# One 512-column product per weight for both parts of x in the input projections, the halves summed on evacuation, and some of VectorE's steps on ScalarE

## The chip, the cores and the metric

The kernel runs on one core of a Trainium2 chip. A core has TensorE for matrix products (into PSUM, 8 banks of 512 fp32 columns), VectorE, ScalarE and GpSimd for the rest, and DMA queues, of which SyncE drives the one that loads weights. The metric is the device time of one execution in microseconds, smaller being better; given is the median of the runs.

## The reference

Two layers over 256 rows of 1024 columns. Each layer projects the rows once, runs three mixers on slices of that projection, projects their joined outputs back, adds and normalises, and then runs a mixture of 32 experts:

```python
def hybrid_mixer(x, w_in, ...):
    p = x @ w_in
    s_z, s_xbc, s_dt, rw, gq, gk, gv, gg, ga = _split(p, IN_SPLITS)
    y_ssd = ssd_mixer(s_z, s_xbc, s_dt, ...)
    y_rwkv = rwkv7_mixer(rw, ...)
    y_gla = gla_mixer(gq, gk, gv, gg, ga, ...)
    y = jnp.concatenate([y_ssd, y_rwkv, y_gla], axis=-1).astype(x.dtype)
    return y @ w_out
...
    for i in range(DEPTH):
        mix = hybrid_mixer(h, w_in[i], ...)
        h = layer_norm(DEEPNORM_ALPHA * h + mix, ln1_g[i], ln1_b[i])
        ffn = hierarchical_moe(h, ...)
        h = layer_norm(DEEPNORM_ALPHA * h + ffn, ln2_g[i], ln2_b[i])
```

The ssd mixer runs a short convolution over its slice (`xbc`) and then a chunked scan with decays exp(min(a_i − a_j, 0)); the rwkv mixer a delta rule, whose chunks are solved with a Neumann series of 32x32 blocks; the gla mixer linear attention with decays from a log sigmoid divided by 16.

## The kernel before

All is fp32, and the products of the mixer keep nearly fp32's accuracy with fp32r operands: each operand is split in a high and a low part (`hi`, a copy on ScalarE rounded to fp32r, and `lo`, the difference, on VectorE), and three products, hi·hi, hi·lo and lo·hi, add up in one PSUM tile (`mm3`, lines 437 to 439). For the rows x, transposed, this is done once a layer (`transposed`, tiles `xh` and `xl`). For a weight it is done in pieces of 128x1024, the tiles `wparts`: the cast on ScalarE (line 143, where every ScalarE operation is recorded) and the difference on VectorE (L411). Three pieces are prepared ahead (`NA`), and there are five buffers (`hring`).

The mixer of a layer is written as three streams of work. Stream r is the rwkv mixer, which starts with the projections lrq and k. Stream s, called attend, holds the gates and decays of the other two (`prep`), the ssd scan (`ssd`, `ssd_out`) and the linear attention (`linear`). Stream d holds the other projections in the order r, v, bc, x0, x1, gk, gv, gg, z0, z1 (`dense`), and then the four output projections (`out_proj`), each of which works in 512 columns. A hand-written clock takes turns between the streams, by the cost that each `yield` states; on the order so written a scheduler lays its own. The result is one fixed order for each engine, with the streams' steps mixed; each engine works through its own order and waits at an instruction until its operands are there.

A projection (`proj`, L542) computes 256 output channels as two halves m of 128, each with 8 steps of 128 inputs; weight pieces are stationary and x moves, 256 columns at a time. Both halves go to one PSUM bank. Halves are read from there by `shift` (L565, the token shift), by `conv` (one ScalarE step and three VectorE steps, L888, for each half), by the gates, or by a copy. For gv the roles are turned: x is stationary and the weights move. The first half of lrq is done apart, in 24 products in another order (L551); it is not touched. The PSUM banks are dealt by stream: three for r, three for d, two for s.

The names that come up later: L659 and L661 form the matrix of the Neumann series; L662 to L665 mask and transpose it into `TM` and `TA`; L765 and L770 are the products of the series, 64 blocks of 32x32 each, with `XY` (L766) and `TM` (L771, L772) evacuated between them on VectorE. L967 and L968 are the cumulative sums of ssd's decays, from `adt`; `cr` (L971) is split from them, `nacs` (L972) is minus the sums in the other layout. `E` (L1041, L1042) is the clamped difference of the sums, taken from PSUM. `zz`, `cum`, `Q` and `QD` (L980 to L995) are the decays of the linear attention and its queries laid out block by block. `po` (L951 to L955) is a polynomial over a 128x16 tile.

After the mixer come the experts. Their weights, 1 MB a transfer, are streamed by SyncE's queue, in order, into tiles of three kinds of buffers; a transfer whose buffer the mixer still holds makes the queue wait (L460).

## Time and profile before

| | |
|---|---|
| time, median of 3 runs (lowest, highest) | 1261.02 us (1260.43, 1264.49) |
| the profiled execution: its time, its span | 1262.9 us, 1261.1 us |
| busy share of the span: TensorE, weight loads, VectorE, ScalarE | 82%, 40%, 29%, 21% |
| DMA queue of SyncE | 439.10 MB, 87.5% of the span |

The shares over the span mix two kinds of stages: the two mixers, in which TensorE and VectorE work, and the two expert parts, in which the DMA engines do. So the stages are read one by one. Start times of TensorE's products are what to read; their ends are modelled, and a busy TensorE is not one at its peak. A row's idle time in brackets names the engine that ended it.

### The profile page before, as it was taken

What the parts mean: (1) busy time and instruction counts of PE and PEld (TensorE: products, weight loads), DVE (VectorE), ACT (ScalarE), POOL (GpSimd) and SP (SyncE); (2) the same over time, 40 slices, a digit from 0 to 9 for tenths busy, and PEclk for the clock granted to TensorE, in tenths of its full rate; (3) what the DMA queues carried; (4) which work ended last, traced back from release to release, by engine and by line L of the source; (5) the groups of instructions that cost most, each with busy time, mean ns of one, the idle gap of its engine ahead of it and who ended that gap; (6) DMA issues with size and microseconds to landing.
All of it is one profiled execution on the core that took longest, in us unless ns stands there. A gap on an engine that the chain in (4) does not pass through costs nothing. (4 is left out here: it accounts for less than half of the span.)

```text
span 1261.1 us, 17850 instructions
## 1 busy us (share of the span) xinstructions
PE 1035.7 (82%) x7497; PEld 506.8 (40%) x7497; DVE 370.1 (29%) x874; ACT 260.5 (21%) x450; POOL 54.0 (4%) x83
## 2 busy tenths in 40 slices
PE   5999998787868777777779999986887787687876
PEld 4899773231223112111268987632312221131211
DVE  5889851010011001000079887411000110010003
ACT  4645541010101000000055463410101010000100
POOL 3011000000000000000001210000000000000001
PEclk9999999998999889988889999999989989888988
DMA  9443789999999999999983356999999999999996
GB/s 309 124 153 120 281 334 392 421 422 420 422 420 422 420 422 421 421 421 367 383 245 111 127 192 244 343 420 422 421 421 421 421 421 421 421 421 420 422 421 222
DMA packets 103003, 443.16 MB, mean 351 GB/s; under 512 B 14080, under 2 KB 39040, under 8 KB 57088
## 3 DMA queue, kind: packets, MB, share of 16 engines
q1 hardware_dynamic: 100928, 439.10, 87.5%
q10 hardware_dynamic: 1856, 2.79, 0.7%
q8 instruction: 63, 1.03, 0.3%
q14 instruction: 28, 0.23, 0.0%
q0 software_dynamic: 128, 0.01, 0.0%
HBM read 440.82 MB, written 1.05 MB: 350 GB/s over the span
## 5 line engine op out<-in xcount | busy, mean ns | idle before, releaser
L1508 PE MATMUL ps<-wslot,xg 128*32 128x512 f32 x768 | 293.8, 678 | 52.9 <-DMA wslot<-in_w_up_dram 39.2
L1508 PE MATMUL ps<-wring,xg 128*32 128x512 f32 x744 | 280.0, 683 | 44.4 <-DMA wring<-in_w_up_dram 38.7
L1508 PE MATMUL ps<-wwide,xg 128*32 128x512 f32 x456 | 221.8, 688 | 34.7 <-DMA wwide<-in_w_up_dram 22.8
L1514 DVE TENSOR_TENSOR hh<-ps,hh 128x256 f32<-128x256 f32 x32 | 12.1, 420 | 509.5 <-PE ps L1508 509.5
L1544 PE MATMUL ps<-wring,hT 128*32 128x512 f32 x384 | 139.1, 603 | 7.9 <-DMA wring<-in_w_down_dram 7.9
L1508 PEld LDWEIGHTS ps<-wslot,xg 128*32 128x32 f32 x768 | 61.3, 121 | 175.2 <-issue 77.0
L1544 PE MATMUL ps<-wslot,hT 128*32 128x512 f32 x320 | 121.4, 610 | 6.9 <-DMA wslot<-in_w_down_dram 6.9
L1508 PEld LDWEIGHTS ps<-wring,xg 128*32 128x32 f32 x744 | 58.4, 122 | 136.9 <-DMA wring<-in_w_up_dram 69.1
L437 PE MATMUL ps<-xh,wparts 128*128 128x256 f32 x320 | 95.0, 297 | 0.0
L1558 DVE SCALAR_TENSOR_TENSOR yy<-ps,gs,yy 128x512 fp32r<-128x512 f32 x32 | 24.0, 751 | 230.2 <-ACT yy L143 226.9
L438 PE MATMUL ps<-xl,wparts 128*128 128x256 f32 x320 | 91.1, 285 | 0.0
L439 PE MATMUL ps<-xh,wparts 128*128 128x256 f32 x320 | 91.1, 286 | 0.0
L1544 PE MATMUL ps<-wwide,hT 128*32 128x512 f32 x192 | 87.7, 608 | 2.1 <-DMA wwide<-in_w_down_dram 2.1
L411 DVE TENSOR_TENSOR wparts<-wslot,wparts 128x1024 fp32r<-128x1024 f32 x62 | 76.7, 1243 | 15.3 <-ACT wparts L143 14.7
L143 ACT ACTIVATE hT<-ps 128x256 f32<-128x256 f32 x32 | 12.3, 383 | 319.4 <-PE ps L1530 319.4
L143 ACT ACTIVATE wparts<-wslot 128x1024 fp32r<-128x1024 f32 x62 | 64.8, 1053 | 58.3 <-PE ps L439 39.6
L1508 PEld LDWEIGHTS ps<-wwide,xg 128*32 128x32 f32 x456 | 43.4, 122 | 82.6 <-DMA wwide<-in_w_up_dram 40.2
L143 ACT ACTIVATE yy<-ps,gs 128x512 fp32r<-128x512 f32 x32 | 22.0, 687 | 210.9 <-PE ps L1544 195.5
L437 PEld LDWEIGHTS ps<-xh,wparts 128*128 128x128 f32 x320 | 61.2, 191 | 4.9 <-issue 2.1
L438 PEld LDWEIGHTS ps<-xl,wparts 128*128 128x128 f32 x320 | 61.2, 191 | 1.1 <-issue 0.9
L439 PEld LDWEIGHTS ps<-xh,wparts 128*128 128x128 f32 x320 | 60.9, 191 | 0.9 <-issue 0.6
L143 ACT ACTIVATE hh<-ps 128x512 f32<-128x512 f32 x16 | 9.6, 597 | 226.5 <-PE ps L1508 135.5
(385 smaller groups left out, 1318.1 us busy)
## 6 DMA issues: line engine op xcount, KB each, us to landing
wring<-in_w_up_dram SPq DMA_DIRECT2D x51, 1024.0 KB, 19.8
wslot<-in_w_gate_dram SPq DMA_DIRECT2D x50, 1024.0 KB, 19.8
wring<-in_w_down_dram SPq DMA_DIRECT2D x48, 1024.0 KB, 19.8
wslot<-in_w_up_dram SPq DMA_DIRECT2D x46, 1024.0 KB, 19.8
wring<-in_w_gate_dram SPq DMA_DIRECT2D x42, 1024.0 KB, 19.8
wslot<-in_w_down_dram SPq DMA_DIRECT2D x40, 1024.0 KB, 19.8
wwide<-in_w_gate_dram SPq DMA_DIRECT2D x30, 1024.0 KB, 19.8
wwide<-in_w_up_dram SPq DMA_DIRECT2D x27, 1024.0 KB, 19.8
```

What stands on the lines that cost most here:

```text
L143: i = nc.scalar.activation(out, in_, func, **kw)
L411: i = V.tensor_tensor(out=lo.bitcast(F32R), in0=w, in1=hi, op=OP.subtract)
L437: return (mm(out, lhsT=lhs[0], rhs=rhs[0], start=start, stop=False), mm(out, lhsT=lhs[0], rhs=rhs[1], start=False, stop=False), mm(out, lh ...
L438: mm(out, lhsT=lhs[0], rhs=rhs[1], start=False, stop=False),
L439: mm(out, lhsT=lhs[1], rhs=rhs[0], start=False, stop=stop))
L1508: mm(pp_[es], lhsT=xg[k // 2][:, k % 2, o + es.start:o + es.stop], rhs=Wx[j][k // 4][k % 4], start=(k == 0), stop=(k == 7))
L1514: V.tensor_tensor(out=hh[:, w], in0=pu[:, w], in1=hh[:, w], op=OP.mult)
L1544: mm(py[n][es], lhsT=hT[:, k, es], rhs=Wd[j][k // 2][k % 2 * 2 + n], start=(k == 0), stop=(k == 3))
L1558: V.scalar_tensor_tensor(yl.bitcast(F32R), py, gs, yh, op0=OP.mult, op1=OP.subtract)
```

## The change

The high and low parts of x now lie side by side, so that both can move past one weight as 512 columns. In `proj` each step is one product of 512 columns, w_hi · [x_hi | x_lo], into a whole bank (L564 in the new file), and one of 256, w_lo · x_hi, into the bank's first half (L561 or L563). So each half of a projection has a bank `q` of its own; its second half of columns is copied out on ScalarE and added to the first on VectorE (L572), into half m of the projection's first bank, from which all goes on as before. The tile for the copy is the one that `shift`, `conv` and the gates write next. For q and gk the sum is the final tile. gv goes the same way with its weight parts moving. The output projections are unchanged.

On top of this, steps of VectorE go to ScalarE: `f` and `lg` (scaling by a column), the clamp of `E` (as Relu of the negated difference, with the sign put right in the exponential), the spreading of `QD` (one product on VectorE, eight copies on ScalarE). The polynomial takes 9 steps for 16, the division of `zz` by 16 moves into the exponentials, and a mask over `st` is one step for four. The costs that the clock knows are set to 0.3 for 0.33 and 2.4 for 2.6.

```diff
-        hi, lo = ([v[:, kq * 512:(kq + 1) * 512].rearrange("p (a b) -> p a b", a=2) for kq in range(4)]
-                  for v in (wide("xh"), wide("xl")))
+
+        xx = [v[:, i * 1024:(i + 1) * 1024].rearrange("p (h a b) -> p h a b", h=2, a=2)
+              for v in (wide("xa"), wide("xb")) for i in range(2)]
+        hi, lo = ([v[:, i] for v in xx] for i in range(2))
...
-        def proj(nm, nm_=2):
-
-            p = ps(2, 256)
+        def proj(nm, nm_=2, room=None, join=None):
+
+            p = d = None
             for m in range(nm_):
                 wp = W.parts(nm, m)
+                q = ps(2, 256)
+                p = p or q
...
                 for k in range(8):
-                    mm3(p[:, m, :], [a[:, k] for a in wp], xT[k], k == 0, k == 7)
+                    if k:
+                        mm(q[:, 0], lhsT=wp[1][:, k - 1], rhs=xT[k - 1][0], start=False, stop=False)
+                    if k == 7:
+                        mm(q[:, 0], lhsT=wp[1][:, k], rhs=xT[k][0], start=False, stop=False)
+                    mm(q, lhsT=wp[0][:, k], rhs=xT[k][3], start=(k == 0), stop=(k == 7))
                     if k % GR == GR - 1:
-                        yield 0.33 * GR, 0, 1
-            return p
+                        yield 0.3 * GR, 0, 1
+                if join:
+                    join(q)
+                    continue
+                d = d or room()
+                act(d[:, m], q[:, 1], AF.Copy)
+                V.tensor_tensor(out=p[:, m], in0=q[:, 0], in1=d[:, m], op=OP.add)
+            return p, d
...
+            def join_q(q):
+                act(qT, q[:, 1], AF.Copy, scale=32.0 ** -0.5)
+                V.scalar_tensor_tensor(qT, q[:, 0], 32.0 ** -0.5, qT, op0=OP.mult, op1=OP.add)
...
-                V.tensor_scalar(f[:, q], ath[:, q], DP[:, l, 11 + q:12 + q], DP[:, l, 13 + q:14 + q],
-                                op0=OP.mult, op1=OP.add)
+                act(f[:, q], ath[:, q], AF.Identity, scale=DP[:, l, 11 + q:12 + q], bias=DP[:, l, 13 + q:14 + q])
...
-                    V.tensor_scalar(q2(lg)[:, q], gr[:, q], p_(l, "lng", q), None, op0=OP.mult)
+                    act(q2(lg)[:, q], gr[:, q], AF.Copy, scale=p_(l, "lng", q))
...
-        def conv(p, j0):
-            a = w512(2, 256, name="cv")
+        def conv(p, a, j0):
...
+                        q = ps(2, 256)
                         for k in range(8):
-                            mm3(pv[:, t], [a[:, t * 128:(t + 1) * 128] for a in xT[k][:2]],
-                                [a[:, k % 4] for a in wv[k // 4]], k == 0, k == 7)
-                        yield 2.6, 0
-                    sh["vg"] = vg = w512(2, 256, name="vg")
-                    act(vg, pv, AF.Copy)
+                            w = wv[k // 4]
+                            mm(q, lhsT=xT[k][0][:, ts], rhs=w[2][:, :, k % 4], start=(k == 0), stop=(k == 7))
+                            if k < 7:
+                                for j in (6, 7) if k == 6 else (k,):
+                                    mm(q[:, 0], lhsT=xT[j][1][:, ts], rhs=wv[j // 4][0][:, j % 4], start=False, stop=False)
+                        vg = vg or w512(2, 256, name="vg")
+                        act(vg[:, t], q[:, 1], AF.Copy)
+                        V.tensor_tensor(out=vg[:, t], in0=q[:, 0], in1=vg[:, t], op=OP.add)
+                        yield 2.4, 0
...
-            V.tensor_scalar(po, z2, 2.0 / 17, 2.0 / 15, op0=OP.mult, op1=OP.add)
-            for m in (13, 11, 9, 7, 5, 3, 1):
-                V.tensor_tensor(out=po, in0=po, in1=z2, op=OP.mult)
-                V.tensor_scalar(po, po, 2.0 / m, None, op0=OP.add)
-            V.tensor_tensor(out=po, in0=po, in1=z_, op=OP.mult)
+            V.tensor_scalar(po, z2, 2.0 / 17, None, op0=OP.mult)
+            for m in (15, 13, 11, 9, 7, 5, 3):
+                V.scalar_tensor_tensor(po, po, 2.0 / m, z2, op0=OP.add, op1=OP.mult)
+            V.scalar_tensor_tensor(po, po, 2.0, z_, op0=OP.add, op1=OP.mult)
...
-            V.tensor_scalar(zz, zz, 1.0 / 16, None, op0=OP.mult)
...
-            act(Q, Q, AF.Exp)
-            for hd in range(4):
-                hs = slice(hd * 32, hd * 32 + 32)
-                for b in range(2):
-                    V.tensor_tensor(out=QD[b][hs, :, hd, :], in0=Q[hs, 4 * b:4 * b + 4],
-                                    in1=sh["qT"][hs, 128 * b:128 * b + 128].rearrange("p (b i) -> p b i", b=4), op=OP.mult)
+            act(Q, Q, AF.Exp, scale=1.0 / 16)
+            V.tensor_tensor(out=Q, in0=Q, in1=sh["qT"].rearrange("p (b i) -> p b i", b=8), op=OP.mult)
+            for b in range(2):
+                for hd in range(4):
+                    hs = slice(hd * 32, hd * 32 + 32)
+                    act(QD[b][hs, :, hd, :], Q[hs, 4 * b:4 * b + 4], AF.Copy)
...
-                    V.tensor_scalar(e[:, 0:256], p[:, hh, :], nacs[:, 0, hd:hd + 1], 0.0, op0=OP.add, op1=OP.min)
-                    V.tensor_scalar(e[:, 256:384], p[:, hh, 128:256], nacs[:, 1, hd:hd + 1], 0.0, op0=OP.add, op1=OP.min)
-                    act(e, e, AF.Exp)
+
+                    act(e[:, 0:256], p[:, hh, :], AF.Relu, scale=-1.0, bias=acs[:, 0, hd:hd + 1])
+                    act(e[:, 256:384], p[:, hh, 128:256], AF.Relu, scale=-1.0, bias=acs[:, 1, hd:hd + 1])
+                    act(e, e, AF.Exp, scale=-1.0)
```

How the order moves, at the two places that the prediction speaks of, both in layer 0.

VectorE, before, where the Neumann series begins: the mask that yields `TM` (L663) and its transpose (L665), between them and ahead of them the split of `cr` and the steps of `zz`; `rv` is a token shift.

```order
L971 TENSOR_TENSOR cr<-ps,cr 32x256 [waits Activation_49]
L565 SCALAR_TENSOR_TENSOR rv<-ps,P,rv 128x255
L662 TENSOR_TENSOR TM<-ps,CM 128x256 [waits PE_49]
L664 STREAM_TRANSPOSE TA<-ps 128x256
L980 SCALAR_TENSOR_TENSOR zz<-zz,za 128x256 [waits Activation_49]
L663 TENSOR_TENSOR TM<-TM,CM 128x256 [waits DVE_49]
L981 TENSOR_SCALAR zz<-zz 128x256 [waits DVE_49]
L665 STREAM_TRANSPOSE TM<-TM 128x256 [waits DVE_49]
```

VectorE, after, the same place (L1002 is `cr`, L681 the mask, L683 the transpose, L414 a weight piece's low part, L1011 `zz`):

```order
L580 SCALAR_TENSOR_TENSOR rv<-ps,P,rv 128x255 [waits Activation_49]
L1002 TENSOR_TENSOR cr<-ps,cr 32x256 [waits Activation_49]
L681 TENSOR_TENSOR TM<-TM,CM 128x256 [waits DVE_49]
L414 TENSOR_TENSOR wparts<-wslot,wparts 128x1024 [waits DMAHW6_49]
L683 STREAM_TRANSPOSE TM<-TM 128x256 [waits DVE_49]
L1011 SCALAR_TENSOR_TENSOR zz<-zz,za 128x256 [waits Activation_49]
```

A weight piece stands between mask and transpose now, and mask and transpose stand behind `cr` with no step of `zz` between.

TensorE, before, where projection x1 and the Neumann series meet: the second product of a series step, XY with TM (L770), and projection products (L437 to L439) around it; 12 of these products follow before the next L765.

```order
L437 MATMUL ps<-xh,wparts 128x256
L438 MATMUL ps<-xl,wparts 128x256
L770 MATMUL ps<-XY,TM 32x32 [waits DVE_49]
L770 MATMUL ps<-XY,TM 32x32 x31
L439 MATMUL ps<-xh,wparts 128x256
L437 MATMUL ps<-xh,wparts 128x256
```

TensorE, after (L788 is the old L770, L783 the old L765; the L564 in the middle is the first product of projection x1, into a bank that has just come free):

```order
L788 MATMUL ps<-XY,TM 32x32 [waits DVE_49]
L788 MATMUL ps<-XY,TM 32x32 x31
L564 MATMUL ps<-xa,wparts 128x512 [waits DVE_49,Activation_49]
L561 MATMUL ps<-xa,wparts 128x256
L564 MATMUL ps<-xa,wparts 128x512
L783 MATMUL ps<-TM,TA 32x32 [waits DVE_49]
```

The projection's first product stands right behind the series' block and waits for a bank, and three projection products stand before the next block, in place of twelve.

VectorE, before, at the same place: the steps of `conv` (L888, the last of a half has 253 columns), XY and TM of the series, and a weight piece.

```order
L888 SCALAR_TENSOR_TENSOR cv<-ps,P,cv 128x254 [waits DVE_49]
L766 TENSOR_TENSOR XY<-ps,CM 128x256 [waits PE_49]
L888 SCALAR_TENSOR_TENSOR cv<-ps,P,cv 128x253 [waits DVE_49]
L411 TENSOR_TENSOR wparts<-wslot,wparts 128x1024 [waits DMAHW7_49,Activation_49]
L888 SCALAR_TENSOR_TENSOR cv<-ps,P,cv 128x255 [waits Activation_49]
L771 TENSOR_TENSOR TM<-ps,TM 128x256 [waits PE_49]
L888 SCALAR_TENSOR_TENSOR cv<-ps,P,cv 128x254 [waits DVE_49]
L772 STREAM_TRANSPOSE TM<-TM 128x256 [waits DVE_49]
L888 SCALAR_TENSOR_TENSOR cv<-ps,P,cv 128x253 [waits DVE_49]
```

VectorE, after (L784 is XY, L905 `conv`, L414 a weight piece, L789 and L790 are TM):

```order
L784 TENSOR_TENSOR XY<-ps,CM 128x256 [waits PE_49]
L905 SCALAR_TENSOR_TENSOR cv<-ps,P,cv 128x254 [waits DVE_49]
L414 TENSOR_TENSOR wparts<-wslot,wparts 128x1024 [waits DMAHW0_49]
L905 SCALAR_TENSOR_TENSOR cv<-ps,P,cv 128x253 [waits DVE_49]
L789 TENSOR_TENSOR TM<-ps,TM 128x256 [waits PE_49]
L414 TENSOR_TENSOR wparts<-wslot,wparts 128x1024 [waits Activation_49]
L790 STREAM_TRANSPOSE TM<-TM 128x256 [waits DVE_49]
```

One weight piece now stands between the last two steps of `conv`, and a second between TM and its transpose.

## Rows read from the trace of the kernel before

**Rows 1.** Busy time by stretches: start and end, then length, then busy time of each engine with its number of instructions; the granted clock of TensorE, the DMA engines' share and rate. Two stretches of layer 0's mixer, one of its experts.

```profile
core 0: us, PE busy (x) PEld busy (x) DVE busy (x) ACT busy (x) POOL busy (x), PEclk, DMA share, GB/s
50.00:77.00 27.00, 26.40 (x608) 23.93 (x607) 24.24 (x58) 13.29 (x22) 2.91 (x6) 1.00 0.41 135
125.00:165.00 40.00, 39.50 (x332) 30.98 (x330) 32.72 (x75) 18.74 (x31) 0.70 (x1) 1.00 0.73 267
200.00:590.00 390.00, 300.94 (x1559) 93.37 (x1553) 29.71 (x80) 29.87 (x61) 0.26 (x1) 0.95 1.01 421
```

**Rows 2.** Waits of SyncE's DMA queue from 100 to 210 us, by line and what ended them: in total, times, longest.

```profile
SPq L460 <- DVE wparts L411: 24.4, 4, 8.7
SPq L460 <- PE ps L439: 19.8, 6, 7.2
```

**Rows 3.** TensorE's timeline from 101.6 to 104.9 us: start, length, instruction. The end of a run of projection products (seven left out between the first two rows), products of the other streams, the start of the next run.

```profile
101.67 0.28 PE L437 MATMUL ps<-xh,wparts 128*128 128x256 f32 x1
...
102.63 0.28 PE L439 MATMUL ps<-xh,wparts 128*128 128x256 f32 x1
102.84 0.88 PE L1053 MATMUL ps<-ssdE,xdt 128*64 128x128 f32 x12
...
104.23 0.50 PE L1036 MATMUL ps<-cr,SEL 64*128 64x256 f32 x2
104.65 0.38 PE L437 MATMUL ps<-xh,wparts 128*128 128x256 f32 x1
104.87 0.28 PE L438 MATMUL ps<-xl,wparts 128*128 128x256 f32 x1
```

**Rows 4.** TensorE's timeline in an output projection: the first and the last of 18 products in a row.

```profile
161.00 0.40 PE L437 MATMUL ps<-wparts,yh 128*128 128x512 f32 x1
...
164.97 0.39 PE L439 MATMUL ps<-wparts,yl 128*128 128x512 f32 x1
```

**Rows 5.** VectorE's groups by line and shape in layer 0's mixer (20 to 165 us): count, busy us, mean ns of one, idle before.

```profile
L1041 DVE TENSOR_SCALAR ssdE<-ps,nacs 128x256 f32<-128x256 f32 x8 | 3.8, 476 | 0.3 <-PE ps L1036 0.3
L1042 DVE TENSOR_SCALAR ssdE<-ps,nacs 128x128 f32<-128x128 f32 x8 | 2.7, 339 | 0.0
L995 DVE TENSOR_TENSOR QD<-Q,qT 32x128 f32<-32x128 f32 x8 | 1.9, 278 | 0.0
L626 DVE TENSOR_SCALAR f<-ath,DP 128x256 f32<-128x256 f32 x2 | 0.8, 409 | 0.0
L953 DVE TENSOR_TENSOR po<-po,z 128x16 f32<-128x16 f32 x7 | 1.2, 170 | 0.1
L981 DVE TENSOR_SCALAR zz<-zz 128x256 f32<-128x256 f32 x1 | 0.7, 718 | 0.0
L766 DVE TENSOR_TENSOR XY<-ps,CM 128x256 f32<-128x256 f32 x4 | 1.6, 412 | 0.0
```

**Rows 6.** ScalarE's groups in the same stretch: a plain copy from PSUM, and one with a scale by a column.

```profile
L143 ACT ACTIVATE AZ<-ps 128x256 f32<-128x256 f32 x4 | 1.4, 376 | 1.1 <-PE ps L693 1.1
L143 ACT ACTIVATE rv<-ps,DP 128x256 f32<-128x256 f32 x4 | 1.9, 475 | 3.4 <-PE ps L439 1.8 <-DVE rv L565 1.6
```

**Rows 7.** Timelines where the Neumann series begins: TensorE's L968 and the start of what follows, then VectorE's `cr` and the transpose that ends the chain.

```profile
54.26 0.62 PE L968 MATMUL ps<-CM,adt 128*32 128x128 f32 x4
54.81 0.30 PE L661 MATMUL ps<-bh,AR 64*32 64x64 f32 x2
...
55.32 0.41 DVE L971 TENSOR_TENSOR cr<-ps,cr 32x256 fp32r<-32x256 f32 x1 [0.77 <-ACT cr L143]
58.44 0.43 DVE L665 STREAM_TRANSPOSE TM<-TM 128x256 f32<-128x256 f32 x1
```

**Rows 8.** Timelines around x0's convolution: VectorE from 68.1 us, then TensorE from 70.2 us.

```profile
68.06 1.21 DVE L411 TENSOR_TENSOR wparts<-wslot,wparts 128x1024 fp32r<-128x1024 f32 x1
69.19 0.47 DVE L888 SCALAR_TENSOR_TENSOR cv<-ps,P,cv 128x254 f32<-128x254 f32 x1
69.58 0.41 DVE L766 TENSOR_TENSOR XY<-ps,CM 128x256 f32<-128x256 f32 x1
69.91 0.47 DVE L888 SCALAR_TENSOR_TENSOR cv<-ps,P,cv 128x253 f32<-128x253 f32 x1
...
70.22 1.11 PE L770 MATMUL ps<-XY,TM 32*32 32x32 f32 x64
71.25 0.38 PE L439 MATMUL ps<-xh,wparts 128*128 128x256 f32 x1
```

**Rows 9.** Timelines at two waits of TensorE: in layer 0 for `adt`; in layer 1 for TM, VectorE's row in the middle and TensorE's last.

```profile
51.24 0.28 PE L437 MATMUL ps<-xh,wparts 128*128 128x256 f32 x1
51.99 0.47 PE L967 MATMUL ps<-adt,CM 128*128 128x8 f32 x3 [0.47 <-DVE adt L959]
...
689.37 1.98 DVE L995 TENSOR_TENSOR QD<-Q,qT 32x128 f32<-32x128 f32 x8
...
691.25 0.28 PE L437 MATMUL ps<-xh,wparts 128*128 128x256 f32 x1
692.29 0.47 PE L765 MATMUL ps<-TM,TA 32*32 32x32 f32 x18 [0.77 <-DVE TM L771]
```

**Rows 10.** ScalarE's timeline: a weight cast that had waited for TensorE, and the instruction after it.

```profile
69.37 1.06 ACT L143 ACTIVATE wparts<-wslot 128x1024 fp32r<-128x1024 f32 x1 [5.00 <-PE ps L439]
70.42 0.56 ACT L143 ACTIVATE cv<-ps,P 128x256 f32<-128x256 f32 x1
```

More of the change, by code (lines that the diff above doesn't have):

```diff
@@ L571, in rwkv @@
                 yield from small_proj()
-            p = yield from proj("lrq")
+            qT = w256(256, name="qT", tag="s")
+            def join_q(q):
+                act(qT, q[:, 1], AF.Copy, scale=32.0 ** -0.5)
+                V.scalar_tensor_tensor(qT, q[:, 0], 32.0 ** -0.5, qT, op0=OP.mult, op1=OP.add)
+            p, _ = yield from proj("lrq", join=join_q)
             if SP == 1:
@@ new lines, in dense, with join_k @@
+                        vg = vg or w512(2, 256, name="vg")
+                        act(vg[:, t], q[:, 1], AF.Copy)
+                        V.tensor_tensor(out=vg[:, t], in0=q[:, 0], in1=vg[:, t], op=OP.add)
+                        yield 2.4, 0
+                    sh["vg"] = vg
+                    continue
+                if nm == "gk":
+                    kT = w512(256, name="kT", tag="r")
+                    def join_k(q):
+                        act(kT, q[:, 1], AF.Copy)
+                        V.tensor_tensor(out=kT, in0=q[:, 0], in1=kT, op=OP.add)
+                    yield from proj(nm, 1, join=join_k)
+                    sh["kT"] = kT
+                    next(aff, None)
+                    continue
```

48 lines of the change are left out of this document (22 added, 26 removed).

## The prediction

> **What bounds the kernel now.** I read first the busy time by stretches [rows 1]. In a mixer (about 20 to 165 us, and again from 644 to 790 us) TensorE is busy nearly all of 50–77 and 125–165 us at a granted clock of 1.00, while the DMA share is 0.41 and 0.73. VectorE is close behind: 24.24 of 27 us, against ScalarE's 13.29. From 200 to 590 us it is the other way round: DMA share 1.01 at 421 GB/s, so the expert part goes at the pace of the weight stream and nothing of this change is in it. The two are tied by the DMA queue on SyncE [rows 2]: between 100 and 210 us it waits for weight parts that VectorE or TensorE must let go. So I take a microsecond lost or won in a mixer as one at the end: time = 1261.02 + what the two mixers lose or gain. The profiled run took 1262.9 us for a span of 1261.1, 1.9 above the median of the runs; the sum is a difference, and I put it on both.
>
> **TensorE's own work.** A layer has 22 half-projections that change (q and gk, and both halves of k, r, v, bc, x0, x1, gv, gg, z0, z1), 8 steps each: 176 steps. Now a step is three products of 256 columns; in a run they start 0.12 us apart (eight pitches from 101.67 to 102.63) [rows 3], 0.36 a step. After, it is one of 512 and one of 256. Products of 512 columns with a weight of their own stand in the output projection: 17 pitches in 3.97 us, 0.2335 each [rows 4]. So a step is 0.3535, and 176 × −0.0065 = −1.1 us a layer. The bounds are 0 (nothing saved) and −3.4: at best the products cost what their columns alone would, by the slope between the two rows, 0.1135 for 256 columns, 0.3405 a step; one fixed part of 0.0065 a step is what I take as saved. Second, such runs are broken into by other products. Entering one costs 0.22 between its first two products (104.65 to 104.87) and leaving it 0.21 (102.63 to 102.84) [rows 3], 0.1 over the pitch each. The new order has 27 runs a layer ahead of the output projection where the old had 31: 4 × 0.2 = −0.8. Together **−1.9 us a layer**, if TensorE never waits.
>
> The Trainium skill, page TensorE: Matmul & The Clock Gate, section Back-to-back issue gap, gives N/2.4 + 2.5 ns between products, by which joining two products of 256 saves 2.5 ns; 176 of them are 0.4 us in place of 1.1, and the sum would be 1.4 us higher for two layers. The trace's 120 and 233.5 ns lie above the page's 109 and 216, and the rows decide.
>
> **VectorE's and ScalarE's work**, a layer. VectorE gets 22 joins, each a sum of two 128x256 tiles, one in PSUM: 0.412 us as L766 [rows 5], +9.1. It loses: ssd's E, 8 × 0.476 + 8 × 0.339 = 6.5; QD, 8 × 0.278 less one product of 0.41, 1.8; f 2 × 0.409 and lg about the same, 1.5; the small polynomial, 7 × 0.17 = 1.2; the 1/16 of zz 0.7. That is −11.7, so **about −2.6 net**; st's three wide products for twelve narrow I count at nothing. ScalarE gets the copies of the second half, 0.376 each as AZ [rows 6] (22, three copies fall away): +7; E's 16 clamps at 0.38 to 0.475, +6.8; f and lg 4 × 0.475 = 1.9; QD's 8 copies, whose form no row has: between 0.2 and 0.4 by AZ, 3. **About +19** of 145 us. ScalarE was at half; alone this costs nothing, its cover being TensorE's 145 us. If the cover fails, the price is in the second rival.
>
> The Trainium skill, page ScalarE: Activation LUTs, section Rules for kernel authors, wants relu, max, add and mul on VectorE, which speaks against E's move. Here the rows of the same tile from PSUM are equal (476 ns on VectorE, 475 with pointer operands on ScalarE), so the move costs no engine time in total; by the page's factor of up to about 3, which it gives for bf16, E would come off VectorE at 2.2 in place of 6.5, VectorE would end heavier by 1.7, and the first rival below would have nothing to stand on.
>
> **Where TensorE waits.** TensorE, VectorE and ScalarE each work strictly in order, so I walked the new order against the durations. Two places come out badly, in both layers.
>
> Place one, the first Neumann product (old L765, new L783). Its operand TM comes off VectorE. Before, some 30 projection products lay behind the products that feed it; now TM's mask stands behind `cr` (L1002), and a weight part (L414, 1.13 us) has come between mask and transpose. From L999's start the chain is 1.06 to `cr` (54.26 to 55.32), 0.41, then mask 0.33, part 1.13, transpose 0.43 [rows 7, 8]: 3.4 us with the hand-over. TensorE has L999's block, 0.55, and nine projection products, 5 × 0.233 + 4 × 0.12 + 0.1: 2.3. **Wait 1.1.**
>
> Place two, the first product of x1 (L564 after L788) and the Neumann product after it. A projection now fills two banks of the three with tag d, p and the second q. With x0's two, the next to come free is bc's, and that is read until the last of conv's three steps on VectorE. That step now stands behind a weight part: after XY (L784) come a conv step 0.39, a part 1.13, the conv step 0.39. XY itself 0.33: x1 starts 2.4 after XY did. TensorE has only the 32-wide block of L788, 1.03 long (70.22 to 71.25), started about 0.46 after XY: wait 0.9 [rows 8]. Then three products, 0.7, against TM 0.33, another weight part 1.13, transpose 0.43: wait about 1.1. **Sum 2.0.** Behind the waiting product stands all of TensorE; VectorE isn't held by it for long, since its own next work is parts.
>
> Both walks use the order as it stands, and if the queues arrive a microsecond apart from what I think, a wait of this size vanishes or doubles: bounds 0 and 6.2 a layer. I take 3.1, since before's own waits of this kind, with the same sort of order, came out near 1.0: TensorE loses 0.75 us from 51.24 to 51.99 (to `adt`, behind VectorE's polynomial) and 1.04 from 691.25 to 692.29 (TM behind the eight QD products) [rows 9]. These two should go, since the polynomial is shorter by 1.2 and QD's 1.98 leaves VectorE: −0.6 in layer 0, −0.9 in layer 1, after the pitch of 0.12.
>
> Sum: layer 0, −1.9 + 3.1 − 0.6 = +0.6; layer 1, −1.9 + 3.1 − 0.9 = +0.3. **+0.9 us: 1261.9** (profiled run 1263.8).
>
> **Rivals.**
>
> *The waits don't come* (faster). VectorE is 2.6 us lighter by the end of a layer and may arrive early at both places; the waits of before then go and the saving stands: 2 × −1.9 − 0.6 − 0.9 = −5.3, **1255.7**. For it: the waits of before are few although VectorE was as full. Against it: place two has a weight part on either side of the conv step, and the joins come before it.
>
> *ScalarE's queue* (slower). Each join begins with a copy on ScalarE, where weight casts stand that wait for TensorE to release a buffer: one stood 5.00 us for TensorE, and the next instruction on ScalarE started 1.05 after it [rows 10]. A copy behind such a cast starts only when TensorE has passed a later product and the cast is done. With three banks and two taken per projection, TensorE then stands for about one cast, 1.05, at the next bank. Five projections a layer (gv, x0, gg, z0, z1) open a bank so closely on another: 2 × 5 × 1.05 = 10.5 above my sum, **1272.4**. It decides from two such places a layer on (2 × 2 × 1.05 + 0.9 = +5.1). Before, a projection had one bank of the three, and a late evacuation cost nothing. Against it: a half takes 2.8 us, longer than cast, copy and join (1.05 + 0.38 + 0.41).
>
> *Weight loads set the pace.* The loads are busy 23.93 of 27 us [rows 1]. If a step's 0.36 were three loads of 0.12, dropping one would save 176 × 0.12 = 21 us a layer: **1219**. Against it: a product of 512 columns with a load of its own takes 0.23, near twice one of 256 [rows 4], so columns set it. The Trainium skill, page Perfetto Trace Analysis, section Identifying the Most-Contended Engine, judges TensorE's headroom by LDWEIGHTS busy share and not by matmul busy share, which would put its weight here; the 0.23 speaks against it.
>
> That the change does not do what it says is hardly open: the order has the 512-column products and the joins in both layers. If the weight stream hid the mixer's end, the sum would come out at no change, inside my own case.
>
> **How the numbers follow.** A measurement tells about 0.3%, 3.8 us, from no change: 1257.2 to 1264.8. My case 0.47 (with the new waits between 1.2 and 5 us a layer, 1258.1 to 1265.7), the waits that don't come 0.25, ScalarE's queue 0.26, the loads 0.02. Faster: 0.19 of the first rival, 0.05 of mine, 0.02: 0.26. Slower: 0.24 of the queue, 0.06 of mine: 0.30. Same: 0.44. For 8 in 10 the range reaches past the first rival, with 1.4 more from streaming in each layer (its bound is 2.3 more), to 1253, and to the queue's five places, 1272; left out are the loads, streaming near its bound, and a queue at more places.
>
> **What would show it.** In the profile after: steps of two products 0.35 us apart; TensorE's idle at L783's first block and at x1's first L564 of about 1.1, 0.9 and 1.1, ended by VectorE's TM, cv and TM; none at `adt` (L998) or behind QD; VectorE's mixer busy time lower by 2 to 3 us, ScalarE's higher by 19 a layer; the full 421 GB/s reached within a microsecond of before. I am wrong if waits on ScalarE's copies end TensorE's idle time at the projections' first products (the queue), if a step is under 0.33 (the loads), or if the mixer gains or loses more than 4 us and the end does not follow.

## The result and the profile after

The kernel after took **1269.63 us** (median of 7 runs, 1266.8 to 1271.03), the kernel before beside it 1261.02 (1260.37 to 1264.49): a ratio of 1.0058 [1.0045, 1.0072], 8.6 us slower. The profiled run took 1271.03 us with a span of 1269.2, 8.1 more than the span before. Two runs of later kernels took far longer than their others (2164 and 1393 us, unexplained); the ratios leave them out, the medians count them.

Where it went is read by the starts of the same products in the two traces. The last product of layer 0's output projection starts at 167.23 us before and 169.34 after (+2.1), the first projection product of layer 1 at 644.19 and 644.50 (+0.3), the last output projection of layer 1 at 791.34 and 797.53 (+6.2), and the last four expert products from 1249.46 and from 1255.31 (+5.85). So two mixers lost 2.1 and 5.9, the end of layer 0's experts gave 1.8 back, and 2.3 more came behind the start of the last expert products.

First the busy time by stretches, to be held against [rows 1], then two stretches behind the waits shown below. The columns are those of [rows 1].

```profile
core 0: us, PE busy (x) PEld busy (x) DVE busy (x) ACT busy (x) POOL busy (x), PEclk, DMA share, GB/s
50.00:77.00 27.00, 24.63 (x503) 19.92 (x502) 24.77 (x51) 16.67 (x34) 3.17 (x6) 0.99 0.54 168
125.00:165.00 40.00, 39.79 (x337) 31.27 (x336) 33.27 (x68) 20.31 (x35) 0.68 (x1) 1.00 0.74 264
200.00:590.00 390.00, 305.45 (x1570) 94.71 (x1570) 30.46 (x83) 29.69 (x62) 0.26 (x1) 0.93 1.01 421
...
78.00:82.00 4.00, 4.00 (x74) 3.45 (x69) 2.13 (x6) 0.56 (x1) 2.50 (x2) 0.77 0.62 243
...
704.00:708.00 4.00, 4.00 (x64) 3.39 (x61) 1.96 (x5) 0.51 (x1) 2.07 (x2) 0.50 0.43 175
```

The expert stretch is unchanged at 421 GB/s. New are the last two rows: TensorE is busy for all of the 4 us, but at a clock of 0.77 and of 0.50; 0.50 is its lower level, 1.2 GHz, for the whole stretch. The granted clock fell at 76.4 us for 3.4 us in layer 0 and at 701.1 us for 10.2 us in layer 1; before, it never fell inside a mixer. Half of 13.6 us is 6.8 us of TensorE's time, 1.7 and 5.1.

What TensorE did ahead of the first fall stands in its timeline. L564 and L561 are projection products (512 and 256 columns), L788 and L783 the Neumann series, L723 the product of AR with bh.

```profile
62.79 0.30 PE L723 MATMUL ps<-AR,bh 64*64 64x64 f32 x2 [0.96 <-DVE rb L1017]
...
68.20 0.40 PE L564 MATMUL ps<-xa,wparts 128*128 128x512 f32 x1
68.43 0.28 PE L561 MATMUL ps<-xa,wparts 128*128 128x256 f32 x1
68.55 0.40 PE L564 MATMUL ps<-xa,wparts 128*128 128x512 f32 x1
...
71.67 0.39 PE L564 MATMUL ps<-xb,wparts 128*128 128x512 f32 x1
72.42 1.11 PE L788 MATMUL ps<-XY,TM 32*32 32x32 f32 x64 [0.36 <-DVE XY L784]
74.43 0.47 PE L564 MATMUL ps<-xa,wparts 128*128 128x512 f32 x1 [0.90 <-DVE cv L905]
...
75.17 1.11 PE L783 MATMUL ps<-TM,TA 32*32 32x32 f32 x64
76.21 0.40 PE L561 MATMUL ps<-xa,wparts 128*128 128x256 f32 x1
76.43 0.60 PE L564 MATMUL ps<-xa,wparts 128*128 128x512 f32 x1
76.83 0.41 PE L561 MATMUL ps<-xa,wparts 128*128 128x256 f32 x1
77.04 0.63 PE L564 MATMUL ps<-xa,wparts 128*128 128x512 f32 x1
```

A step of two products takes 0.35 us (68.20 to 68.55), as forecast. Then come two short waits, 0.36 for XY and 0.90 for the bank of projection x1, with L788's 32-wide products between them. Two microseconds later the same products are slow: 0.61 a step (76.43 to 77.04) in place of 0.35. VectorE's timeline there shows who was late.

```profile
71.95 0.42 DVE L784 TENSOR_TENSOR XY<-ps,CM 128x256 f32<-128x256 f32 x1
72.28 0.47 DVE L905 SCALAR_TENSOR_TENSOR cv<-ps,P,cv 128x254 f32<-128x254 f32 x1
72.67 1.22 DVE L414 TENSOR_TENSOR wparts<-wslot,wparts 128x1024 fp32r<-128x1024 f32 x1
73.80 0.48 DVE L905 SCALAR_TENSOR_TENSOR cv<-ps,P,cv 128x253 f32<-128x253 f32 x1
74.19 0.42 DVE L789 TENSOR_TENSOR TM<-ps,TM 128x256 f32<-128x256 f32 x1
74.52 1.22 DVE L414 TENSOR_TENSOR wparts<-wslot,wparts 128x1024 fp32r<-128x1024 f32 x1
75.66 0.44 DVE L790 STREAM_TRANSPOSE TM<-TM 128x256 f32<-128x256 f32 x1
```

The weight part stands between the last two steps of `conv`, and the bank comes free when the second of them ends, at 74.28. TM's product starts at 75.17, ahead of the transpose at 75.66: it needs L789 alone.

TensorE's waits in layer 1's mixer (640 to 800 us; total, times, longest) name the same ones and that of the layer's first projection:

```profile
PE ps L556 <- ACT xb L143: 2.0, 1, 2.0
PE ps L723 <- DVE rb L1017: 1.0, 1, 1.0
PE ps L564 <- DVE cv L905: 0.9, 1, 0.9
...
PE ps L788 <- DVE XY L784: 0.4, 1, 0.4
```

L556 is the first projection of the layer, whose operand is made while it waits. Before, 16 narrow products of `small_proj` (L875) filled this place; now they come some 14 us later.

The groups that answer to [rows 5, 6], in layer 0's mixer: a join, then on ScalarE the copy for it, the clamps of E and the copies of QD.

```profile
L572 DVE TENSOR_TENSOR ps<-ps,cv 128x256 f32<-128x256 f32 x6 | 2.5, 422 | 0.1
...
L143 ACT ACTIVATE ssdE<-ps,acs 128x256 f32<-128x256 f32 x8 | 3.8, 475 | 1.7 <-PE ps L1084 1.0 <-PE ps L1066 0.6
L143 ACT ACTIVATE ssdE<-ps,acs 128x128 f32<-128x128 f32 x8 | 2.9, 368 | 0.0
L143 ACT ACTIVATE QD<-Q 32x128 f32<-32x128 f32 x8 | 2.5, 307 | 1.1 <-DVE Q L1022 1.0
L143 ACT ACTIVATE cv<-ps 128x256 f32<-128x256 f32 x6 | 2.0, 375 | 0.7 <-PE ps L564 0.7
```

At the very end VectorE's timeline has the last expert evacuation and the first instruction behind the loop's branch (L1619), and then that instruction in the kernel before:

```profile
1255.29 0.75 DVE L1588 SCALAR_TENSOR_TENSOR yy<-ps,gs,yy 128x512 fp32r<-128x512 f32 x1 [3.09 <-ACTq L1619]
1258.92 0.70 DVE L250 BATCH_NORM_STATS2 bst<-ps 128x6 f32<-128x512 f32 x1 [2.88 <-DVEq L1619]
...
1250.79 0.70 DVE L250 BATCH_NORM_STATS2 bst<-ps 128x6 f32<-128x512 f32 x1 [0.59 <-PE ps L1561]
```

2.88 us idle here, put down to VectorE's own queue at that branch; before, 0.59. These are the 2.3 us: from the start of the last four expert products to the end of the span it is 13.9 us, and 11.7 before.

### The profile page after: what moved, and what is told of

The parts are those of the page before. It is cut to its first block, busy times and chain, and to the rows that moved or that the text cites. A ratio compares the mean times of both kernels' runs of the same rounds, so it can differ in the third digit from the quotient of the medians.

```text
span 1269.2 us, 17216 instructions
## 1 busy us (share of the span) xinstructions
PE 1039.1 (82%) x7145; PEld 492.2 (39%) x7145; DVE 371.7 (29%) x830; ACT 288.5 (23%) x544; POOL 55.0 (4%) x83
## 5 line engine op out<-in xcount | busy, mean ns | idle before, releaser
L1544 DVE TENSOR_TENSOR hh<-ps,hh 128x256 f32<-128x256 f32 x32 | 12.1, 420 | 500.9 <-PE ps L1538 500.9
L1574 PE MATMUL ps<-wring,hT 128*32 128x512 f32 x384 | 142.3, 613 | 10.6 <-DMA wring<-in_w_down_dram 10.6
L414 DVE TENSOR_TENSOR wparts<-wslot,wparts 128x1024 fp32r<-128x1024 f32 x62 | 77.6, 1256 | 15.6 <-ACT wparts L143 15.6
L564 PE MATMUL ps<-xa,wparts 128*128 128x512 f32 x160 | 62.2, 417 | 2.1 <-DVE cv L905 1.8
L564 PE MATMUL ps<-xb,wparts 128*128 128x512 f32 x160 | 61.9, 406 | 0.0
L1591 PE MATMUL ps<-yy,gT 128*128 128x512 f32 x128 | 47.8, 456 | 9.0 <-ACT yy L143 6.8
L1574 PEld LDWEIGHTS ps<-wring,hT 128*32 128x32 f32 x384 | 27.5, 110 | 58.6 <-issue 31.9
L561 PE MATMUL ps<-xa,wparts 128*128 128x256 f32 x160 | 48.3, 302 | 0.0
L1519 PE MATMUL ps<-oh,z 128*128 128x256 f32 x256 | 39.6, 295 | 7.5 <-DVE xg L1528 5.1
```

The costliest lines, as they stand in the source:

```text
L414: i = V.tensor_tensor(out=lo.bitcast(F32R), in0=w, in1=hi, op=OP.subtract)
L561: mm(q[:, 0], lhsT=wp[1][:, k - 1], rhs=xT[k - 1][0], start=False, stop=False)
L564: mm(q, lhsT=wp[0][:, k], rhs=xT[k][3], start=(k == 0), stop=(k == 7))
L1519: mm(p[:, i, :], lhsT=zp[a][t][k // 4][:, k % 4 * 128:k % 4 * 128 + 128], rhs=oh[:, t].rearrange("p a b -> p (a b)"), start=(t + a == 0), ...
L1544: V.tensor_tensor(out=hh[:, w], in0=pu[:, w], in1=hh[:, w], op=OP.mult)
L1574: mm(py[n][es], lhsT=hT[:, k, es], rhs=Wd[j][k // 2][k % 2 * 2 + n], start=(k == 0), stop=(k == 3))
```

## The experiments

The theory after the result, A: the clock falls because of the two waits at x1's start, and TensorE's time at 1.2 GHz is most of the loss. Its rivals, spelled out in the expectations: the waits and the later weight stream cost by themselves, or the moved work (ScalarE's) costs, not the merged products. No kernel leaves work out; the added products add zeros, and the added copies feed nothing.

**The wait filled.** Six products of 512 columns with a 64-column weight of zeros, added to x0's own sum, where TensorE would stand for XY and then for the bank.

```diff
...
+                    if nm == "x0" and m == 1 and k == 7:
+                        for _ in range(6):
+                            mm(q[0:64], lhsT=Z[0].bitcast(F32R), rhs=xT[k][3], start=False, stop=False)
                     mm(q, lhsT=wp[0][:, k], rhs=xT[k][3], start=(k == 0), stop=(k == 7))
```

> The changed kernel, with six products of 512 columns and a weight of zeros (64 columns) put into the sum of x0's second half just ahead of its last step: 6 x 0.2335 = 1.4 us more work for TensorE, at the place where it waits 0.5 us for XY and then 1.1 us for x1's bank; results are the same. Theory A (the clock): the waits there are what lets TensorE's granted clock fall to 1.2 GHz right after, for 3.4 us in layer 0 and 10.2 us in layer 1, which costs half of these times, 1.7 + 5.1 = 6.8 of the 8.6 us that the change lost. Then with the wait filled by work the clock stays at 1.00 in both mixers and the time comes to 1262.5 to 1264.5, though TensorE does more. Theory B (the wide products themselves lower the clock) and theory C (ScalarE's copies and moves cost the time): the clock falls as before or the loss stays elsewhere, and the time is 1269 to 1272.

1263.65 us, 1.0015 [1.0004, 1.0026] of before (1261.66 in these runs): some 6 us of the 8.6 are back, although TensorE has more to do. The profiled run, 1267.93 us, was the longest of the twelve. Its timeline (L796 is the old L788, L572 the first product of x1), and its stretches:

```profile
70.84 1.54 PE L571 MATMUL ps<-xb,zt 128*64 128x512 f32 x6
72.22 0.39 PE L572 MATMUL ps<-xb,wparts 128*128 128x512 f32 x1
72.54 1.11 PE L796 MATMUL ps<-XY,TM 32*32 32x32 f32 x64
73.60 0.47 PE L572 MATMUL ps<-xa,wparts 128*128 128x512 f32 x1
```

```profile
76.00:80.00 4.00, 4.00 (x85) 3.32 (x84) 3.50 (x9) 0.76 (x2) 2.11 (x2) 1.00 0.78 275
...
706.00:710.00 4.00, 4.00 (x80) 3.44 (x81) 3.40 (x8) 1.51 (x2) 1.34 (x2) 1.00 0.32 125
```

No wait is left at L796 and x1. The products fill the wait and do not shorten it: x1 starts 2.47 us after XY (71.13), as in after (2.48). The clock stays at 1.00 behind them in both layers, and layer 0's output projection ends 0.2 us behind before's (167.44), where it was 2.1. The wait at AR·bh is still there and no fall follows it. One fall is left, 3.4 us from 648.0, behind layer 1's start, where TensorE waited 2.32 us.

**The control.** The same six products in a later half, z0's, behind the place.

```diff
...
+                    if nm == "z0" and m == 1 and k == 7:
```

> A control for filler: the same six products with a weight of zeros, but in the sum of z0's second half, 40 us later, where TensorE does not wait. The order around x1 is that of the changed kernel. Theory A: the waits for XY and for x1's bank stand as before, the clock falls right after them, and the time is that of the changed kernel with up to 2 x 1.4 us on top: 1269 to 1273. If any extra work or a changed order does what filler did, it comes to 1262 to 1266.

1270.89 us, 1.0064 [1.0049, 1.0079] (before 1262.47 in these runs). The waits at x1 are as in after (0.35 and 0.90), and the clock fell behind them in both layers, for 10.2 and 6.8 us:

```profile
76.00:80.00 4.00, 4.00 (x44) 3.07 (x40) 1.80 (x4) 0.80 (x2) 1.94 (x2) 0.50 0.89 286
...
706.00:710.00 4.00, 4.00 (x51) 3.40 (x48) 2.87 (x7) 0.00 (x0) 1.42 (x2) 0.52 0.31 126
```

So the place of the six products decides, not their number. A holds for the falls behind x1, and in the medians for most of the loss.

**The weight part behind conv.** An edge in the order puts the part behind conv's last step, so that x1's bank comes free earlier.

```diff
...
-                    V.scalar_tensor_tensor(a[:, m, o:256], p[:, m, 0:256 - o], w(k), a[:, m, o:256],
-                                           op0=OP.mult, op1=OP.add)
+                    conved[0] = V.scalar_tensor_tensor(a[:, m, o:256], p[:, m, 0:256 - o], w(k), a[:, m, o:256],
+                                                       op0=OP.mult, op1=OP.add)
...
+        elif conved[0] is not None:
+            after(i, conved[0])
```

> The changed kernel with an order edge: a weight part's difference on VectorE comes after the last convolution step written ahead of it, so that no weight part stands between the last steps of conv(bc), which free the bank of x1's first product. Theory A: TensorE's wait at x1's first product falls from 1.1 us to under 0.3 and the clock stays up there: 1262 to 1265, unless weight parts that come later make TensorE wait as long at the next half. Theory B: clock still falls, 1268 to 1271.

1267.86 us, 1.0052 [1.0033, 1.0071]. The clock did what A says: no wait at x1, 1.00 in both mixers, and their last output products stand at 168.49 and 791.99, 1.3 and 0.7 behind before. The time did not follow; A's time is missed. New waits (PV 0.9, KB 0.9) have come, and the profiled run (1267.57 us, span 4.5 over before's) shows where the rest went. Just behind layer 1's mixer, in the products between mixer and experts (L167), the clock falls for 3.4 us; first this kernel, then before:

```profile
796.00:800.00 4.00, 4.00 (x18) 3.34 (x18) 3.50 (x18) 4.00 (x7) 0.00 (x0) 0.67 1.06 423
...
796.00:800.00 4.00, 4.00 (x21) 3.39 (x21) 3.79 (x18) 3.43 (x5) 0.00 (x0) 1.00 1.05 425
```

All later work is 1.6 us later by it (+0.7 ahead, +2.3 behind), and the branch at the end, idle 2.67 in place of 0.59, adds 2.1. The same fall, between 796 and 804 us, stands in four traces of kernels that follow, with the same 1.6 us: the moves alone, the moves alone with copies in one group, after with spread copies, and the first partial merge. Before, after, the filler and the control do not have it, so a part of what separates the kernels does not lie in the mixers.

**The merge without the moves.** All moves of work undone: E, QD, f, lg, the polynomial, the 1/16 of zz, and st's mask with them.

```diff
-                act(f[:, q], ath[:, q], AF.Identity, scale=DP[:, l, 11 + q:12 + q], bias=DP[:, l, 13 + q:14 + q])
+                V.tensor_scalar(f[:, q], ath[:, q], DP[:, l, 11 + q:12 + q], DP[:, l, 13 + q:14 + q],
+                                op0=OP.mult, op1=OP.add)
...
-                    act(e[:, 0:256], p[:, hh, :], AF.Relu, scale=-1.0, bias=acs[:, 0, hd:hd + 1])
+                    V.tensor_scalar(e[:, 0:256], p[:, hh, :], nacs[:, 0, hd:hd + 1], 0.0, op0=OP.add, op1=OP.min)
...
```

> The changed kernel with VectorE's steps back on VectorE (f, lg, clamp of E, QD, polynomial, zz, st as in the kernel before): the merged products and their joins alone. Its order has the same place as the changed kernel: x1's first product behind conv's last step and a weight part. Theory A: the wait of 1 us and the fall of the clock stay, and VectorE carries 9 us more a layer than before: 1269 to 1276. Theory C (the moves to ScalarE cost the time): the loss goes with them, 1259 to 1263.

1285.68 us, 1.0178 [1.0154, 1.0203], far above what A named. TensorE's longest waits from 20 to 180 us:

```profile
PE ps L789 <- DVE XY L785: 1.4, 1, 1.4
PE ps L724 <- DVE AR L720: 1.4, 1, 1.4
PE ps L564 <- DVE cv L906: 0.9, 1, 0.9
PE ps L840 <- ACT PQ L143: 0.8, 1, 0.8
PE ps L1130 <- DVE KB L1122: 0.7, 1, 0.7
```

All but one are for VectorE, and the clock fell six times in the mixers, for 41 us in all, which costs 20. At the end of layer 1's mixer the profiled run is 26.6 us behind before's; the other 6 are not laid out here, the waits shown sum to 5.2 in layer 0 alone. The moves to ScalarE are what makes the joins bearable. That the moves cost is refuted from this side.

**The moves without the merge.** The same edits made in the kernel before.

```diff
-                V.tensor_scalar(f[:, q], ath[:, q], DP[:, l, 11 + q:12 + q], DP[:, l, 13 + q:14 + q],
-                                op0=OP.mult, op1=OP.add)
+                act(f[:, q], ath[:, q], AF.Identity, scale=DP[:, l, 11 + q:12 + q], bias=DP[:, l, 13 + q:14 + q])
...
```

> The kernel before with only the moves from VectorE (f, lg, clamp of E and QD to ScalarE, the shorter polynomial, zz and st); products of 256 columns as before, one bank for a projection. Theory A: no projection waits for a bank, the waits of before for adt and behind QD go (0.6 + 0.9 us), the clock stays at 1.00 in the mixers: 1259 to 1261. Theory C: ScalarE's added 12 us a layer hold up weight casts and evacuations: 1264 to 1269.

1263.96 us, 1.0019 [1.0010, 1.0028], between the ranges of A and C: no gain, no fall of the clock inside a mixer. The mixers end level with before's (+0.3 and −0.4 us): the waits of [rows 9] are gone, but one of 1.4 us for `sn` (L842) is new in each layer. Then the clock falls behind layer 1's mixer (795.9 us, as above). One more thing is off here: VectorE's branch at the end of layer 0 took 4.50 us, from its start to VectorE's next event, against 0.57 at the end of the program.

**The branch.** VectorE's two branches, at the ends of the layers, are instructions 434 and 986 of its list before. After, the filler, its control and the kernel with the part behind conv have 412 and 942, and the second is long; the moves alone have 390 and 898, and the first is long. The merge alone has none of these numbers, and both of its branches are short. Copies of one column into an unused tile, 22 a layer (44 with the moves alone), bring them back to 434 and 986. First in one group:

```diff
+            if q == 2:
+                idle = small(1, "idle")
+                for _ in range((22, 22)[l]):
+                    V.tensor_copy(out=idle, in_=pg[:, 0:1])
```

> The kernel filler with 22 one-column copies on VectorE in each layer's experts (third group of four), so that VectorE's branch over the block for overfull experts stands at the same instruction number as in the kernel before (434 and 986). In the profiles so far this branch took 0.54 us at the end of layer 1 in the kernel before, but 3.04 in the changed kernel, 2.82 in filler and 2.84 in conv_first, which have it at 942. Theory D (where the branch lies in the program decides): the branch takes under 0.6 us again and the time is 1261.0 to 1262.0, that of filler less 2.3. Theory E (other traffic at the end, weights or queues, decides): it stays near 2.8 and the time at 1263 to 1265.

1264.24 us, 1.0024 [1.0013, 1.0036]: the branch is short (0.54) and the time no better than without the copies. (From here on the filler's weight of zeros has 32 columns in place of 64; its six products take as long, 1.55 us.) Between layer 1's mixer and the last expert products the trace loses 2.1 us against before. That the group of copies does it is not shown: below, the filler with spread copies loses 1.6 there, and the second partial merge, with 34 copies in a group, nothing.

> The kernel moves_only with 44 such copies in each layer, its VectorE branches at 434 and 986 as in the kernel before; without them the branch at the end of layer 0 took 4.50 us (0.57 in the kernel before). Theory D: it takes 0.6 us, and the moves alone come to 1259.0 to 1261.0, a gain of 1 to 2 us by the waits for adt and behind QD that go. Theory E: the branch stays at 4 us and the time at 1263 to 1265.

1263.41 us, 1.0002 [0.9986, 1.0018]; both branches short. In this trace the clock fell inside layer 1's mixer, at 758.5 us for 3.4, behind a wait of 1.35 us for `sn`, with no merged product in the kernel. Then the copies were spread over the pieces of the experts:

```diff
+            idle = small(1, "idle")
+            for _ in range((0, 4, 4, 4, 4, 3, 3, 0)[q]):
+                V.tensor_copy(out=idle, in_=hh[:, 0:1])
```

> The changed kernel with 22 one-column copies on VectorE in each layer, spread over six expert groups behind the step that TensorE waits for, so that VectorE's branches stand at 434 and 986. Theory D: the last branch takes 0.54 in place of 3.04 us and the time falls by 2.3 to 2.5, to 1266.5 to 1268. If the branch's length does not reach the end: 1269 to 1270.5.

1265.17 us, 1.0027 [1.0018, 1.0036], some 4 us under after and under D's range. The profiled run, 1268.63 us, was the longest of its eleven and cannot tell why the median gained more than the branch. In it the clock did not fall behind x1 in layer 1, though the waits were there; behind x1 in layer 0 it fell for 10.2 us, and at layer 1's start, 647.1, for 6.8.

> The kernel filler with the copies of after_spread. In filler_pad the branch was short (0.54 us) and yet the time stayed at 1264.2; all 22 copies stood there in one group, ahead of the step that TensorE waits for, and the trace lost 1.5 to 2 us between 820 and 1128 us. If the copies took the gain there, it comes out now: 1261 to 1262.3. If the branch's length does not reach the end: 1263 to 1264.5.

1264.67 us, 1.0022 [1.0012, 1.0032]: the branch 0.54, the clock 1.00 in both mixers, layer 1's mixer 148.65 us from first to last product (147.15 before, 153.03 after), and no gain over the filler alone.

> The kernel moves_only with 44 copies in each layer, spread likewise. Theory D: branch at the end of layer 0 at 0.57 in place of 4.50 us; the moves alone come to 1259.5 to 1261.5, a little ahead of the kernel before. If not: 1263 to 1264.

1264.32 us, 1.0019 [1.0007, 1.0032]: no gain over the moves alone. Of five pairs with the branch cured, one is clearly shorter (after), one by 0.17% with intervals that overlap, three not.

**Part of the merge.** bc, x0 and x1 left in the old form (three products of 256, one bank), then k, r and v as well (10 of 22 half-projections merged); each with copies, in one group, that hold the branches short.

```diff
+            if nm in ("bc", "x0", "x1"):
+                p, d = ps(2, 256), room()
+                for m in range(nm_):
+                    wp = W.parts(nm, m)
+                    for k in range(8):
+                        mm3(p[:, m, :], [a[:, k] for a in wp[:2]], xT[k], k == 0, k == 7)
...
+                return p, d
```

> The changed kernel with the three projections that go into the convolution (bc, x0, x1) back to three products of 256 columns and one bank each; 16 of the 22 halves keep the merged products; 28 copies a layer put the branches at 434 and 986. Theory A: no projection waits for a bank that a convolution holds, the clock stays at 1.00 in both mixers, and the time comes to 1258.5 to 1261.5. If merged products cost time wherever they stand (theory B), the clock falls elsewhere in the mixers and the time is over 1264.

1268.32 us, 1.0050 [1.0033, 1.0066]. The profiled run, 1264.21 us, was the shortest. x1's waits are gone, but TensorE waits three times for AR (0.93, 0.28, 0.26 from 62.1 to 64.6 us) and the clock falls at 66.2 us. That is as B had it: over 1264, with a fall elsewhere.

> As partial_pad, but k, r and v are back to products of 256 too: 10 of 22 halves merged (q, gk, gv, gg, z0, z1), 34 copies a layer for the branches. Theory A: clock at 1.00, less streaming saved (10 x 8 x 0.0065 = 0.5 us a layer in place of 0.8), fewer joins on VectorE before the convolutions and so no wait at AR times bh (1.1 us in the changed kernel): 1258.5 to 1261. Theory B: between partial_pad and the kernel before by the number of merged halves.

1262.71 us, 1.0006 [0.9998, 1.0015]: what twelve merged halves cost is gone, and what ten might save is not seen. The time lies between A's range and B's, an estimate of 1266 (10 of 16 merged halves at the first partial merge's 6.4 us). In its profiled run the clock still fell in layer 0, at 75.2 us for 3.4, behind 1.03 us of idle time in a block of 32-wide products that the profile puts to no engine, and in layer 1 at 645.2, behind 1.10 for a weight cast. No version beat the kernel before.

## Why the prediction was wrong in size

The likeliest case, +0.9 us, missed; 1269.63 lies inside the range, near the price of the rival of ScalarE's queue, but not by its mechanism. That the range holds it is luck: the queue set its upper end, and the likeliest case, with every new wait up to 5 us a layer, ended at 1265.7.

**The step that failed is the price of a wait.** "Where TensorE waits" charges each wait its own length and nothing behind it. Place two's first wait came as forecast: x1 starts 2.48 us after XY (2.4 forecast), idle 0.90, in both layers. Its price was that and, behind it, TensorE at half clock: 1.7 us in layer 0 and 5.1 in layer 1 of the profiled run, where the sum had nothing. Without those 6.8 us layer 0's mixer lost 0.4 and layer 1's 0.8, against the forecast +0.6 and +0.3; that these are near is partly chance, since of the three waits walked one came, and others took the place of two. The filler and its control show this by experiment: with the place filled the clock fell behind it in 0 of 6 mixers (filler, and filler with either set of copies), with both waits there in 7 of 8 (after, control, merge alone, after with spread copies), and some 6 of the 8.6 us went with it. How long a fall lasts varied from 3.4 to 10.2 us with the same waits. That may be a part of why the runs of after spread over 4 us; those of the kernel before, with no such fall in its trace, spread as far.

The Trainium skill, page TensorE: Matmul & The Clock Gate, section A second HAM failure mode: psum-queue depth-cycling, tells of a bf16 kernel in which short idle moments between groups of products, while these cycle through banks, make the clock move between its levels. The traces agree in part: 0.36 for XY and 0.90 for a bank were followed by 0.50 of the clock in 7 of 8 mixers, and other waits as long were not (last section).

**Terms that held.** The step: 0.353 us as forecast; loads did not set the pace. The formula N/2.4 + 2.5 ns that the prediction takes from the Trainium skill, page TensorE: Matmul & The Clock Gate, section Back-to-back issue gap, is given there for a single product by itself, not for a stream of loads and products; nothing in the sum rests on it. The joins 0.422 (0.412 forecast), E's clamps 0.475 and 0.368, QD's copies 0.307 within 0.2 to 0.4. VectorE's busy time from 20 to 165 us went from 122.8 to 120.7, −2.1 (forecast −2.6): the step behind E (L1044, new L1075) takes 0.816 us for 0.691, 1.0 more in all, which the sum did not have, and st takes 0.5 less. ScalarE's added rows sum to about 18 (copies 6.9, E 6.7, f and lg 2.1, QD 2.5; forecast 19); its busy time rose by 14.2, since neighbours overlap. The waits at `adt` and behind QD [rows 9] are gone.

**Terms that failed otherwise.** Place one did not wait: L783 started at 58.15 and its transpose (L683) at 58.75. I had taken the transpose for its operand; the product needs the mask alone. The second wait of place two failed the same way (75.17 against 75.66). [rows 8] did not hold the pair that would have told it. In their place came waits that I had not walked: AR·bh 0.96, layer 1's start 1.98, XY 0.36. The first of them in VectorE's rows:

```profile
59.68 0.43 DVE L1011 SCALAR_TENSOR_TENSOR zz<-zz,za 128x256 f32<-128x256 f32 x1 [0.49 <-ACT za L143]
...
60.35 1.04 DVE L1014 TENSOR_TENSOR_SCAN cum<-C,zz 128x256 f32<-128x256 f32 x1
61.32 1.04 DVE L689 TENSOR_TENSOR kp<-kraw,f 128x512 f32<-128x512 f32 x1
62.28 0.16 DVE L1016 TENSOR_TENSOR rb<-cum 128x8 f32<-128x8 f32 x1
62.37 0.28 DVE L719 TENSOR_TENSOR AR<-rv,ecw 128x128 f32<-128x128 f32 x1
```

`zz` waited 0.49 for ScalarE's `za`, and behind its chain stands AR, which the product reads and which ends at 62.65, 0.14 ahead of TensorE's start. The profile puts the wait down to `rb` (L1017), the next step, which is no operand of the product.

**The rivals.** The waits did come. ScalarE's queue did not: no idle of TensorE at a projection's first product is ended by a ScalarE copy; the bank at x1 waited for VectorE. ScalarE is in it only at `za` and at layer 1's start.

**A microsecond in a mixer as one at the end** is the second step that failed: it held for layer 1, not for layer 0. Microseconds behind the kernel before, in the profiled runs:

| | end of layer 0's mixer | start of layer 1 | end of layer 1's mixer | last expert products | span |
|---|---|---|---|---|---|
| after | +2.1 | +0.3 | +6.2 | +5.9 | +8.1 |
| filler | +0.2 | +0.6 | +3.5 | +3.0 | +5.0 |
| control | +6.4 | +1.1 | +8.3 | +7.6 | +9.7 |
| part behind conv | +1.3 | −1.7 | +0.7 | +2.4 | +4.5 |
| merge alone | +13.0 | +12.1 | +26.6 | +26.6 | +26.6 |

What layer 0's mixer lost, up to 6.4 us, hardly reached layer 1; only the 13.0 of the merge alone did. Of after's 8.1 us, then, 0.3 are left of layer 0, 5.9 come from layer 1's mixer (5.1 of them by the clock), 2.3 from the branch, and layer 1's experts gave 0.4 back. Where layer 0's loss went may in part be the clock again, which is low late in layer 0's experts in every trace: from 600 us on, before for 17.0 us (from 602.9 and from 633.6 us), after for 13.6, in the control for 6.8. Half of the difference is 1.7 and 5.1 us, and 1.8 and 5.3 were got back; the kernel with the part behind conv got 3.0 back where this gives 1.7, so the cause stays open. SyncE's queue still hangs on VectorE's parts:

```profile
SPq L463 <- DVE wparts L414: 29.3, 4, 10.3
```

**The branch and what is open.** In the profiled runs the last branch reaches the end whole: from the start of the last expert products to the end of the span it is 13.7 to 13.9 us in the four kernels where it is long and 11.6 to 11.7 in the other ten. In the medians the pairs with copies do not show it alike; what else changed between them stays open, and so does why the clock falls behind layer 1's mixer in some traces and not in others.

## What to carry to other kernels

A wait that a change puts on TensorE can cost more than its length: look at the granted clock just behind each new wait, and price the stretch at half clock. Compare the starts of the same products at several places, since what one stage loses need not reach the end. When fewer products do the same work, they also fill fewer gaps: filling the gap with idle products, and a control with the same products elsewhere, tells the clock from the wait with two kernels. Check which instruction a product really needs (its start against the supposed operand's end) before walking an order.

## What the runs showed of the hardware

Two waits of TensorE, 0.36 and 0.90 us with 32-wide products between them (1.41 and 0.90 in the merge alone), were followed by its lower clock in 7 of 8 mixers. Of single idle times, 0.97 and 1.02 at AR·bh (filler) were not, 1.38 and 1.44 there (merge alone) and 1.03 within 32-wide products (second partial merge) were; at layer 1's start 2.32 (filler) was, 1.98 (after) and 2.59 (filler with spread copies) were not. So the length alone does not decide, and no run here shows what does.

VectorE's taken branch, from its start to VectorE's next event, took 0.54 to 0.57 us where it was instruction 434 or 986 of its list (in all eight kernels that have it there) and at 412 and 898, but 2.8 to 3.0 at 942 (four kernels) and 4.50 at 390. The Trainium skill, page Runtime: NRT & Kernel Launch, section Instruction fetch mechanics, says that a taken branch whose target lies outside the window at hand waits for a fetch; the runs show that the length goes with the position and not that a fetch is the cause.
